# Joining the in-chunk products of a state-space group into one run of column tiles

## The chip, the cores and the metric

The kernel runs on one core of one Trainium2 chip. The metric is the device time of one launch in microseconds (us). Before the change the median of three runs is 729.46 us (729.12, 729.46 and 731.79).

Engines are named as the profile names them: PE multiplies matrices (PEld is its weight load), DVE is the vector engine, ACT the scalar engine, POOL the engine for general work, SP issues the DMAs. Each engine works through its own queue in order and waits at the head of it for what other engines have to deliver. PE writes into eight PSUM banks of 128 partitions by 512 float32 values.

## The reference, cut to what matters

The reference is a two-layer encoder trunk for 512 tokens of width 1024. Layer 0 is a Mamba-2 mixer, layer 1 is differential attention, and a final RMSNorm ends it. The change is in the state-space scan of layer 0:

```python
def step(state, inp):
    x_c, a_c, b_c, c_c = inp
    acs = jnp.cumsum(a_c, axis=1)
    seg = acs[:, :, None] - acs[:, None, :]
    decay = jnp.exp(jnp.where(causal, seg, -jnp.inf))
    cb = jnp.einsum("blgn,bsgn->blsg", c_c, b_c)
    y_diag = jnp.einsum("blsgr,bsgrp->blgrp", cb[..., None] * decay, x_c)
    y_off = jnp.einsum("blgn,bgrpn->blgrp", c_c, state) * jnp.exp(acs)[..., None]
    to_end = jnp.exp(acs[:, -1:] - acs)
    new_state = (state * jnp.exp(acs[:, -1])[..., None, None]
                 + jnp.einsum("blgn,blgrp->bgrpn", b_c, x_c * to_end[..., None]))
    return new_state, y_diag + y_off
```

There are 8 groups with 4 heads of 64 channels each, and a state of 128. `y_diag` is the part inside a chunk, `y_off` is what the state of earlier chunks adds, and `new_state` carries on. Around it stand a projection to z, x, B, C and dt, a causal convolution of four taps on x, B and C, a gate with a grouped norm, and the output projection.

## The kernel before, in words

**Numbers.** Each large product is split into a high and a low part in float32r and made of three matmuls (`mm3`): high by high, high by low, low by high. ACT writes the high part of a weight tile (`whi`) and DVE the low part (`wlo`). The products of the scan itself are plain float32, which the trace shows as two records for each product.

**The stream of dense work.** `stream_a` yields the projections of layer 0 in the order z0 g0 g1 z1 g2 g3 z2 g4 o0 g5 z3 g6 g7 o1 o2 o3. A `g` item (`group_proj`) makes four tiles `pg{g}_0` to `pg{g}_3` (B, C and the two halves of x of one group) in four PSUM banks with the tag "mm". `conv` then works on each: DVE multiplies by the row scale, ACT starts the sum of the four taps, DVE adds the three other taps out of PSUM (`xc<-pg,prc,xc`, shapes 511, 510 and 509), and ACT applies SiLU. The bank of a `pg` tile is free when its last tap (509) is done; then the next item's first matmul can go into it. An `o` item makes 128x512 tiles `po` in the same four banks, and DVE adds each to the residual `x_tok`.

**The scan.** `ssd(g)` is called when the projection of group g is complete. It works on four chunks of 128 tokens. In order of the program:

- C by B for the four chunks into `pcb`, in the one bank with the tag "long"
- transposes of B (`pbt`) and of x (`pxt`); DVE makes `xdt` (x times dt) and `dx` (the skip term), POOL makes `xe` (weighted to the chunk's end)
- DVE multiplies the four heads of the decay tile `dec` by `pcb`, in place
- the states' products `psA` (chunks 0 and 1) and `psB` (chunk 2); ACT, POOL and DVE make the states `hst` of them
- the products inside the chunks, `pyd`: 32 products of 128x64 by 128x64, two for each chunk and head, because the 128 output rows are written as two column tiles of 64. Chunks 0 and 1 fill the bank `pyd{g}_0`, chunks 2 and 3 fill the bank `pyd{g}_1`; DVE adds each bank to `dx`
- the products with the states (`po1`, `po2`, shown as `po<-hst,xc`), DVE scales them into `tmp`, POOL adds them to `dx` for chunks 1 to 3, DVE multiplies by the gate `zs`, ACT squares with a sum, DVE finds the reciprocal root in about ten steps on 128x4 (`v`, `y_i`, `y_y`, `y_c`), ACT scales, PE transposes into `pyt`, and ACT and DVE split the result into `yh` and `yl` for the output projection

All scan tiles but `pcb` come from three banks with the tag "ss". After an odd group, `decays` prepares the `dec` tiles of the next two groups: a 1 MB broadcast DMA, four subtractions and four triangular selections on POOL, and one exponential on ACT. There are two `dec` buffers, so the one of group g+2 is free when the `pyd` products of group g are done.

**What sets the order.** In layer 0 the order on each engine is not written out. The framework's scheduler places every instruction by priority and by its own estimate of a timeline, and interleaves the scan of one group with the dense stream of the next items. Only where the wrapper `Ordered` is switched on (`T.on`, `V.on`, `A.on`) is an instruction kept in program order against the others so marked. Before the change `T.on` is off through the whole scan; it is on from the end of layer 0.

Of the kernel before, what the change touches and what calls it, by code (L numbers as in the profile page):

```python
# [23 lines left out]
R = 4  # L24
# [39 lines left out]
def trunk(ctx, tc, x, x_t, par, w_dt, w_in, w_out, w_kvqg, w_bo, d_skip, lam_qk, fin_g, out):  # L64
    nc = tc.nc
    V, A, T = (Ordered(tc, e) for e in (nc.vector, nc.scalar, nc.tensor))
# [14 lines left out]
    def ss_bank(name):  # L81
        turns[0] += 1
        tag = "mm" if turns[0] % turns[1] >= 3 else "ss"
        return psum.tile([P, 512], F32, tag=tag, name=name, bufs=3 if tag == "ss" else 4)

    def long_bank(name):
        return psum.tile([P, 512], F32, tag="long", name=name)
# [473 lines left out]
    def ssd(g):  # L561
        bc, cc, x0, x1 = conv_out.pop(g)
        xc = (x0, x1)
        dec, een, _ = decs.pop(g)
# [28 lines left out]
        hst = bp.tile([P, 3, R, HD], F32, tag="hst", name=f"hst{g}")  # L593
        hsf = hst.rearrange("p c h e -> p c (h e)")
        psA = ss_bank(f"psA{g}")
        for c in range(2):
            T.matmul(psA[:, c * 256:(c + 1) * 256], lhsT=bt[:, c, :], rhs=xe[:, c].rearrange("p h e -> p (h e)"), start=True, stop=True)
        A.copy(hsf[:, 0], psA[:, 0:256])
# [6 lines left out]

        ss4 = small.tile([P, NQ], F32, tag="ss4", name=f"ss4{g}")
        tmp = bp.tile([P, NQ, R, HD], F32, tag="tmp", name=f"tmp{g}")
        pyd = []
        for q in range(2):
            pyd.append(ss_bank(f"pyd{g}_{q}"))  # L610
            for c in (2 * q, 2 * q + 1):
                for h in range(R):
                    o = (c % 2) * 256 + h * HD

                    for r in (slice(0, 64), slice(64, 128)):
                        T.matmul(pyd[q][r, o:o + HD], lhsT=dec[:, h, c, r], rhs=xdt[:, c, h, :], start=True, stop=True)
            dq = dx[:, 2 * q:2 * q + 2].rearrange("p c h e -> p c (h e)")
            V.tensor_tensor(out=dq, in0=pyd[q].rearrange("p (c e) -> p c e", c=2), in1=dq, op=ALU.add)
        if g % 2 and g < G - 1:
# [35 lines left out]
    for g in range(G):  # L655
        until(f"g{g}")
        if g < G - 1:
            ssd(g)
        else:
            with tc.high_priority():  # L660
                ssd(g)
# [277 lines left out]
    def half(t, n):  # L939
        hs = slice(n * 512, (n + 1) * 512)  # L940
        return x_tok[:, t, hs], fg[:, hs], ot[t][:, hs], out[t * P:(t + 1) * P, hs]
# [59 lines left out]
    h = DH - 1  # L1001
# [59 lines left out]
    y, f, o, dst = half(3, 0)  # L1061
# [71 lines left out]
```

## Time and profile before

| | |
|---|---|
| median of three runs | 729.46 us |
| the profiled execution | 729.15 us, of which the span from the first to the last instruction is 727.0 us |
| granted TensorE clock | 0.998 |
| PE busy | 713.5 us (98%) |
| DVE, ACT, POOL busy | 528.0, 433.7 and 117.7 us |
| `pyd` products | 512 records from 78.2 to 408.4 us |

A row of the timeline has the start in us, the length in us, engine, source line, operation, output tile and inputs, shapes, the count, and in brackets the idle time before it with what ended it. Records of one kind that follow each other are merged into one row. Matmuls are pipelined, so a row's length is longer than the time until the next one starts: a 128x512 product is 0.40 us long, and the next starts 0.23 us after it. The price of work on PE is therefore read from starts, not from lengths. Nearly every instruction has line 55, the line of the wrapper, so groups are told apart by tile names.

### The profile page before, as it was taken

How to read it: one execution, taken by the hardware profiler on the slowest of the kernel's cores; microseconds unless marked ns; L12 is line 12 of the kernel's file. 1: busy time of each engine (PE TensorE's matmuls, PEld its weight loads, DVE VectorE, ACT ScalarE, POOL GpSimd, SP SyncE). 2: the span in 40 equal slices, each digit the busy share in tenths (PEclk: the TensorE clock that was granted, in tenths of full speed). 3: DMA queues.
4: the chain of work that ended last, by engine and by line, in shares of the span. 5: the costliest groups of instructions: out<-in, count | busy, mean ns of one | idle time of the engine just before them, and what ended most of it. 6: DMA issues, size and time to landing. Idle time of an engine off the chain costs nothing.

```text
span 727.0 us, 10819 instructions
## 1 busy us (share of the span) xinstructions
PE 713.5 (98%) x3989; PEld 593.1 (82%) x3989; DVE 528.0 (73%) x1202; ACT 433.7 (60%) x965; POOL 117.7 (16%) x158
## 2 busy tenths in 40 slices
PE   9999999999999999999999999999999999999996
PEld 7787888888888888887788869888988898889874
DVE  4688964979479668569995846657667857785886
ACT  5948573654735527527534348667766756756566
POOL 0108241412315024150110101000000000000002
PEclk9999999999999999999999999999999999999999
DMA  8634313314133231231122310331221131122003
GB/s 302 233 131 162 116 59 117 117 58 175 58 117 116 95 137 60 91 142 59 59 70 105 116 59 9 117 115 59 94 82 58 59 117 59 59 90 85 29 1 115
DMA packets 12916, 70.86 MB, mean 97 GB/s; under 512 B 1728, under 2 KB 2496, under 8 KB 5312
## 3 DMA queue, kind: packets, MB, share of 16 engines
q1 hardware_dynamic: 12576, 69.90, 26.5%
q8 instruction: 31, 0.51, 0.3%
q10 hardware_dynamic: 288, 0.28, 0.1%
q14 instruction: 21, 0.17, 0.1%
HBM read 68.02 MB, written 2.16 MB: 97 GB/s over the span
## 4 chain that ended last, share of the span: by engine, by line
PE 90%; DVE 7%; ACT 1%; issue 1%; POOL 0%; ACTq 0%; DVEq 0%; POOLq 0%
PE pg L55 21%; PE po L55 14%; PE pz L55 12%; PE pt L55 7%; PE pv L55 6%; PE pq L55 6%; PE pk L55 6%; PE pb L55 3%; PE sc L55 3%; PE pyd L55 2%; PE pc L55 2%; DVE wlo L55 2%; DVE xc L55 2%; PE pyt L55 1%; PE pxt L55 1%; PE psA L55 1%
## 5 line engine op out<-in xcount | busy, mean ns | idle before, releaser
L55 DVE SCALAR_TENSOR_TENSOR wlo<-raw,prm,whi 128x512 fp32r<-128x512 f32 (+1 forms) x256 | 150.4, 633 | 52.7 <-ACT whi L55 51.3
L55 ACT ACTIVATE whi<-raw,prm 128x512 fp32r<-128x512 f32 (+1 forms) x256 | 136.8, 606 | 81.4 <-PE pg L55 30.1
L55 PE MATMUL pg<-a_hi,whi 128*128 128x512 f32 x256 | 103.3, 404 | 1.5 <-DVE y_c L55 1.5
L55 PE MATMUL pg<-a_hi,wlo 128*128 128x512 f32 x256 | 102.3, 402 | 0.0
L55 PE MATMUL pg<-a_lo,whi 128*128 128x512 f32 x256 | 102.3, 400 | 0.0
L55 DVE SCALAR_TENSOR_TENSOR xc<-pg,prc,xc 128x511 f32<-128x511 f32 (+2 forms) x96 | 69.6, 738 | 4.8 <-ACT xc L55 4.4
L55 PEld LDWEIGHTS pg<-a_hi,whi 128*128 128x128 f32 x256 | 48.1, 188 | 13.1 <-issue 1.9
L55 PEld LDWEIGHTS pg<-a_hi,wlo 128*128 128x128 f32 x256 | 48.1, 188 | 11.0
L55 PEld LDWEIGHTS pg<-a_lo,whi 128*128 128x128 f32 x256 | 48.1, 188 | 10.7
L55 PE MATMUL po<-whi,yh 128*128 128x512 f32 x128 | 51.4, 402 | 1.5 <-DVE xc L55 0.8
L55 PE MATMUL po<-wlo,yh 128*128 128x512 f32 x128 | 51.1, 399 | 0.0
L55 PE MATMUL po<-whi,yl 128*128 128x512 f32 x128 | 50.4, 398 | 0.0
L55 PE MATMUL pz<-wlo,a_hi 128*128 128x512 f32 x128 | 50.3, 399 | 0.0
L55 PE MATMUL pz<-whi,a_lo 128*128 128x512 f32 x128 | 49.8, 398 | 0.0
L55 PE MATMUL pz<-whi,a_hi 128*128 128x512 f32 x128 | 49.6, 401 | 0.0
L971 POOL TENSOR_TENSOR ot<-ot,fg 128x512 f32<-128x512 f32 x4 | 5.1, 1289 | 256.9 <-ACT ot L55 256.9
L55 ACT ACTIVATE s<-s,mx 128x128 f32<-128x128 f32 (+3 forms) x64 | 35.5, 556 | 9.6 <-DVE mx L55 9.1
L55 ACT ACTIVATE xc<-pg,prc 128x512 f32<-128x512 f32 x32 | 24.6, 773 | 26.6 <-DVE pg L55 26.5
L589 POOL TENSOR_TENSOR xe<-xdt,tok 128x256 f32<-128x256 f32 x24 | 17.3, 749 | 139.6 <-DVE xdt L55 139.6
L55 DVE CUSTOM_DVE_ANT_0 s<-sc,bias 128x128 f32<-128x128 f32 (+3 forms) x64 | 29.4, 488 | 12.2 <-PE sc L55 11.7
L55 ACT ACTIVATE xc<-xc 128x512 f32<-128x512 f32 x32 | 20.0, 629 | 28.3 <-DVE xc L55 28.2
L55 PE MATMUL pv<-whi,b_hi 128*128 128x256 f32 x128 | 36.6, 286 | 0.0
(243 smaller groups left out, 1719.7 us busy)
## 6 DMA issues: line engine op xcount, KB each, us to landing
raw<-in_w_in SPq DMA_DIRECT2D x23, 1024.0 KB, 4.8
raw<-in_w_kvqg SPq DMA_DIRECT2D x16, 1024.0 KB, 4.8
dec<-acs_d SPq DMA_DIRECT2D x8, 1024.0 KB, 4.8
raw<-in_w_out SPq DMA_DIRECT2D x8, 1024.0 KB, 4.8
raw<-in_w_bo SPq DMA_DIRECT2D x4, 1024.0 KB, 4.8
x_tok<-in_x SPq DMA_DIRECT2D x4, 512.0 KB, 9.3
out<-ot SPq DMA_DIRECT2D x7, 256.0 KB, 2.4
raw<-in_w_in SPq DMA_DIRECT2D x4, 256.0 KB, 5.8
```

The costliest lines, as they stand in the source:

```text
L55: i = op(*args, **kw)
L589: GP.tensor_tensor(out=xe[:, c], in0=xdt[:, c], in1=toe_tok[:, c, hs].unsqueeze(2).to_broadcast([P, R, HD]), op=ALU.mult)
L971: GP.tensor_tensor(out=o, in0=o, in1=f, op=ALU.mult)
```

## The change

The products of `ssd` from `psA` to the last of `pyd` are now kept in program order on PE. The second bank of `pyd` no longer comes from the three "ss" banks but is the "long" bank, which `pcb` has held before in the same group. The chunks are taken in the order 2, 3, 0, 1 and the heads from 3 down to 0, all 32 products behind each other; the two additions to `dx` on DVE come after all of them in the program. No product and no other operation is added or taken away.

```diff
         psA = ss_bank(f"psA{g}")
+        T.on = True
         for c in range(2):
             T.matmul(psA[:, c * 256:(c + 1) * 256], lhsT=bt[:, c, :], rhs=xe[:, c].rearrange("p h e -> p (h e)"), start=True, stop=True)
...
         tmp = bp.tile([P, NQ, R, HD], F32, tag="tmp", name=f"tmp{g}")
-        pyd = []
-        for q in range(2):
-            pyd.append(ss_bank(f"pyd{g}_{q}"))
+
+        pyd = [ss_bank(f"pyd{g}_0"), long_bank(f"pyd{g}_1")]
+        for q in (1, 0):
             for c in (2 * q, 2 * q + 1):
-                for h in range(R):
+                for h in reversed(range(R)):
                     o = (c % 2) * 256 + h * HD
 
                     for r in (slice(0, 64), slice(64, 128)):
                         T.matmul(pyd[q][r, o:o + HD], lhsT=dec[:, h, c, r], rhs=xdt[:, c, h, :], start=True, stop=True)
+        T.on = False
+        for q in range(2):
             dq = dx[:, 2 * q:2 * q + 2].rearrange("p c h e -> p c (h e)")
             V.tensor_tensor(out=dq, in0=pyd[q].rearrange("p (c e) -> p c e", c=2), in1=dq, op=ALU.add)
```

Since the scheduler works with the whole program, the order moves on every engine through layer 0, up to the last transposes of group 7. Three places follow.

On PE in group 6, this is the piece of the difference around the first two tiles of the output projection o1 (`po_0_0`, `po_0_1`); `pg_3` is the last tile of the projection of group 7, and numbers tell one tile from another.

```order
 L55 MATMUL pg_3_3051<-a_hi,wlo_2963 128x512
-L55 MATMUL psB_3109<-xe_3094,bt_3076 128x256
-L55 MATMUL pyd_0_3115<-xdt_3078,dec_2683 64x64 x16
 L55 MATMUL po_0_0_3348<-whi_3054,yh_1539 128x512
 L55 MATMUL po_0_0_3348<-wlo_3055,yh_1539 128x512
```

```order
 L55 MATMUL po_0_0_3348<-whi_3054,yl_1868 128x512
+L55 MATMUL psA_3103<-xe_3094,bt_3076 128x256 x2
+L55 MATMUL psB_3109<-xe_3094,bt_3076 128x256
+L55 MATMUL pyd_1_3116<-xdt_3078,dec_2683 64x64 x16
+L55 MATMUL pyd_0_3115<-xdt_3078,dec_2683 64x64 x16
 L55 MATMUL po_0_1_3498<-whi_3054,yh_1539 128x512
```

```order
 L55 MATMUL po_0_1_3498<-whi_3054,yl_1868 128x512
-L55 MATMUL pcb_3352<-xc_3291,xc_3272 128x128 x4
-L55 MATMUL pyd_1_3133<-xdt_3078,dec_2683 64x64 x16
-L55 MATMUL po_3151<-hst_3102,xc_3003 128x256
 L55 MATMUL po_0_2_3512<-whi_3054,yh_1539 128x512
```

Before, the two halves of `pyd` stood 24 products of `po` apart; now both stand together between `po_0_0` and `po_0_1`, with the states' products ahead of them. In the same stretch the eight transposes `pxt` of group 6 moved from the products of `pg_0` to those of `pg_3`.

On DVE behind group 5, these are the rows from the root of group 5's norm (`v`, `y_i`, `y_y`, `y_c`) to the last tap of the convolution on the first tile of group 6 (`xc_2984<-pg_0_2896`, 509). Before:

```order
L55 TENSOR_TENSOR pg_0_2896<-pg_0_2896,ar_row 128x512
L55 TENSOR_SCALAR v_2741<-ss_2645 128x4
L55 TENSOR_SCALAR y_i<-v_2741 128x4
L55 TENSOR_SCALAR y_y<-y_i 128x4
L55 TENSOR_TENSOR y_c<-y_y,v_2741 128x4
L55 TENSOR_TENSOR y_c<-y_c,y_y 128x4
L55 TENSOR_TENSOR pg_1_2897<-pg_1_2897,ar_row 128x512
L55 SCALAR_TENSOR_TENSOR xc_2984<-pg_0_2896,prc,xc_2984 128x511
L55 SCALAR_TENSOR_TENSOR y_c<-y_c 128x4
L55 SCALAR_TENSOR_TENSOR xc_2984<-pg_0_2896,prc,xc_2984 128x510
L55 SCALAR_TENSOR_TENSOR y_y<-y_c,y_y 128x4
```

and now:

```order
L55 TENSOR_TENSOR pg_0_2896<-pg_0_2896,ar_row 128x512
L55 TENSOR_TENSOR tmp_2646<-po_2725,tok 128x512
L55 SCALAR_TENSOR_TENSOR xc_2984<-pg_0_2896,prc,xc_2984 128x511
L55 SCALAR_TENSOR_TENSOR xc_2984<-pg_0_2896,prc,xc_2984 128x510
L55 TENSOR_TENSOR pg_1_2897<-pg_1_2897,ar_row 128x512
L55 SCALAR_TENSOR_TENSOR xc_2984<-pg_0_2896,prc,xc_2984 128x509
```

Before, a tap of the second tile (`xc_3003`) and then the 509 tap followed the last row shown. Now the 509 tap ends the rows shown, and the root starts behind nine of the twelve taps of group 6.

On ACT at the end of layer 0, this is the piece of the difference from group 7's copy of the first state to its scaling; `tmp,ss<-dx` are the four squares, and `whi_3746` is the weight split of the next layer's first tile.

```order
 L55 COPY hst_3387<-psA_3388 128x256
-L55 ACTIVATE tmp_3399,ss_3398<-dx_3364 128x256 x3
-L55 ACTIVATE whi_3746<-raw_3744,prm 128x256 x5
-L55 ACTIVATE tmp_3399,ss_3398<-dx_3364 128x256
-L55 ACTIVATE whi_3746<-raw_3744,prm 128x256 x3
+L55 ACTIVATE tmp_3399,ss_3398<-dx_3364 128x256 x4
+L55 ACTIVATE whi_3746<-raw_3744,prm 128x256 x8
 L55 ACTIVATE tmp_3399<-dx_3364,y_y 128x256 x4
```

Before, the fourth square stood behind five weight splits; now all four squares come first. On POOL, after groups 0 to 5, the subtractions for the decay tile that becomes free now stand ahead of the second and third addition to `dx` of the same group; before they stood behind them in four of the six.

## The prediction

> **What bounds the kernel now.** I read the page first: the busy shares and the chain of waits.
>
> ```profile
> span 727.0 us, 10819 instructions
> PE 713.5 (98%) x3989; PEld 593.1 (82%) x3989; DVE 528.0 (73%) x1202; ACT 433.7 (60%) x965; POOL 117.7 (16%) x158
> PE 90%; DVE 7%; ACT 1%; issue 1%; POOL 0%; ACTq 0%; DVEq 0%; POOLq 0%
> ```
>
> PE is busy for 98% of the span and holds 90% of the chain. A change can win in two ways only: PE spends less on the same products, or one of its few waits goes. So the second view is the list of what PE waited for.
>
> ```profile
> PE pg L55 <- DVE y_c L55: 1.5, 1, 1.5
> PE po L55 <- DVE xc L55: 0.8, 1, 0.8
> PE pyt L55 <- ACT tmp L55: 0.7, 1, 0.7
> PE pxt L55 <- ACT xc L55: 0.6, 1, 0.6
> PE po L55 <- ACT yh L55: 0.6, 1, 0.6
> ```
>
> These five waits of layer 0 (total, times, longest, all in us) are single events. The fourth lies in group 0, ahead of the first instruction that moves, and the fifth is the way from the last transposes into the last output tiles, whose order is the same. The first three can change.
>
> The third view is the timeline of PE around the `pyd` runs of group 0, with the row of all `pyd` records (length at least, median and most in ns).
>
> ```profile
> 78.24 1.15 PE L55 MATMUL pyd<-xdt,dec 128*64 128x64 f32 x32
> 79.33 0.50 PE L55 MATMUL pg<-a_hi,whi 128*128 128x512 f32 x1
> 79.66 0.40 PE L55 MATMUL pg<-a_lo,whi 128*128 128x512 f32 x1
> ...
> 83.86 0.40 PE L55 MATMUL pg<-a_lo,whi 128*128 128x512 f32 x1
> 84.09 0.40 PE L55 MATMUL pg<-a_hi,wlo 128*128 128x512 f32 x1
> 84.42 1.15 PE L55 MATMUL pyd<-xdt,dec 128*64 128x64 f32 x32
> 85.50 1.56 PE L55 MATMUL po<-hst,xc 128*128 128x256 f32 x6
> ```
>
> ```profile
> L55 PE MATMUL pyd<-xdt,dec x512: 222/222/270, 78.2 to 408.4; 128*64 128x64 f32 x171
> ```
>
> The reader is to see the edges of a run. A 128x512 product is followed by the next after 0.23 us (83.86 to 84.09), but after 0.33 us when a run of `pyd` comes next (84.09 to 84.42). The first product behind a run also takes 0.33 us (79.33 to 79.66).
>
> **The change part by part. First, the run's edges.** The run is 1.15 us long and its last record 0.22 us, so 31 steps take 0.93 us: 0.03 us for one record, 0.96 us for 32. From its start to the next product's start a run takes 1.08 us (84.42 to 85.50), so leaving costs 0.12 us. With 0.10 us on entering and 0.10 us on the first product after it, one run costs 0.32 us beyond its products. The change makes one run of 64 records out of two of 32 in each of eight groups: 8 x 0.32 = 2.6 us. All of it is on PE and nothing hides it. Low end: if the seam in the joined run, where the second bank's first product waits for semaphores anew, costs an entry of 0.10 us, 8 x 0.22 = 1.8 us stay. High end: if a run's first steps are slower than its mean, as one record of 270 ns beside a median of 222 suggests, some 0.05 us more, 3.0 us in all. I take 2.6, since the steps come from the mean of a whole run.
>
> The page "TensorEngine Tiling (Array Packing)" of the Trainium skill, section "Tiling Modes", says that changing the tiling mode drains the TensorE, and changing only the tile does not. By that rule the seam, which keeps the mode, costs nothing, and the saving would be the full price of a run; by the other reading the seam pays an entry. The page has no figure for a drain.
>
> **The second bank and the order of heads** cost nothing if the products never wait for `dec` or for the "long" bank. Group 0 is the tightest: its decay tiles are multiplied by `pcb`, which also empties that bank, long before 78.24.
>
> ```profile
> 65.59 2.48 DVE L55 TENSOR_TENSOR dec<-dec,pcb 128x512 f32<-128x512 f32 x4 [0.78 <-ACT dec L55]
> ```
>
> That ends at 68.07, 10.2 us ahead. Behind the waiting product the whole stream of PE would stand, so the cover matters; it would have to shrink by these 10 us.
>
> **The first wait (PE on the bank of group 6's first tile).** This is the timeline behind group 5, all engines.
>
> ```profile
> 320.94 4.92 POOL L553 TENSOR_TENSOR dec<-dec,tok 128x512 f32<-128x512 f32 x4
> ...
> 322.85 0.69 DVE L55 TENSOR_TENSOR pg<-pg,ar_row 128x512 f32<-128x512 f32 x1
> ...
> 323.89 0.97 DVE L55 TENSOR_SCALAR y_i<-v 128x4 int32<-128x4 int32 x1
> ...
> 324.90 0.98 DVE L55 TENSOR_SCALAR y_y<-y_i 128x4 int32<-128x4 int32 x1
> ...
> 326.97 0.69 DVE L55 TENSOR_TENSOR pg<-pg,ar_row 128x512 f32<-128x512 f32 x1
> ...
> 328.69 0.40 PE L55 MATMUL pg<-a_hi,wlo 128*128 128x512 f32 x1
> ...
> 329.07 1.40 DVE L55 SCALAR_TENSOR_TENSOR xc<-pg,prc,xc 128x511 f32<-128x511 f32 x2
> ...
> 330.62 0.47 PE L55 MATMUL pg<-a_hi,whi 128*128 128x512 f32 x1 [1.53 <-DVE y_c L55]
> ```
>
> PE would have gone on at 328.69 + 0.23 = 328.92 and went on at 330.62: 1.7 us late. The name `y_c` is only the next DVE instruction. What PE needs is the 509 tap of `pg_0`, the second of the two in the row of 329.07, which ends at 330.47. It is late because between the multiply of `pg_0` (to 323.54) and that of `pg_1` (326.97) DVE works 3.4 us on five steps of the norm's root, two of them of nearly 1 us on 128x4 while POOL subtracts. In the changed order these steps stand behind the tap. Behind the multiply of `pg_0` come `tmp`, two taps, the multiply of `pg_1` and the 509 tap: 0.69 + 0.70 + 0.70 + 0.69 + 0.70 = 3.5 us, and 0.2 us because ACT's part of the convolution is a little longer than `tmp`. The tap ends at 323.54 + 3.7 = 327.2, 1.7 us before PE asks. I take the whole 1.7 us as gone. Bounds: 1.7 and 0.0, the latter if POOL's subtractions, which also come earlier now, hold DVE up by the same 3.4 us at the weight splits ahead. What is late instead is the root of group 5; its transposes have moved too, in among the products of group 7's first tile.
>
> **The second wait (PE on the bank of group 7's second tile).**
>
> ```profile
> 355.84 1.02 PE L55 MATMUL psA<-xe,bt 128*128 128x256 f32 x4
> ...
> 361.20 0.40 PE L55 MATMUL po<-whi,yl 128*128 128x512 f32 x1
> 361.56 0.73 DVE L55 SCALAR_TENSOR_TENSOR xc<-pg,prc,xc 128x509 f32<-128x509 f32 x1
> ...
> 362.43 0.47 PE L55 MATMUL po<-whi,yh 128*128 128x512 f32 x1 [0.83 <-DVE xc L55]
> ```
>
> ```profile
> 353.18 1.28 DVE L55 TENSOR_TENSOR pg<-pg,ar_row 128x512 f32<-128x512 f32 x2
> 354.38 4.01 DVE L55 SCALAR_TENSOR_TENSOR xc<-pg,prc,xc 128x511 f32<-128x511 f32 x6
> ```
>
> `po_0_1` was due at 361.43 and started at 362.43, 1.0 us late, behind the tap that ends at 362.29. DVE rows take 0.67 us each here (4.01 / 6). Before, 14 rows follow `pg_1`'s multiply up to that tap, 9.4 us from 353.18. In the changed order DVE has 15 rows there, 10.0 us, but ahead of the multiply only `pg_0`'s, a weight split and two `yl`, 4 x 0.67 = 2.7 us, while PE takes 12 x 0.23 = 2.8 us for `pg_1`: it can take the tile up at once. PE now has between `pg_1` and `po_0_1` 36 products of 0.23 (8.3 us), the states' products (1.3 us, six passes of some 0.22) and both halves of `pyd` (2.0 us), 11.6 us without the eight transposes. That leaves 1.6 us. I take 1.0 us as gone; if DVE is again some 2.5 us late with `pg_1`, 0.9 us come back, so the bounds are 0.1 and 1.0.
>
> **The third wait (the last transposes on group 7's scaling).**
>
> ```profile
> 411.92 1.01 DVE L55 TENSOR_TENSOR tmp<-po,tok 128x256 f32<-128x256 f32 x2
> ...
> 415.46 2.10 ACT L55 ACTIVATE whi<-raw,prm 128x256 fp32r<-128x256 f32 x5
> ...
> 417.46 0.40 ACT L55 ACTIVATE tmp<-dx 128x256 f32<-128x256 f32 x1
> ...
> 420.40 0.40 PE L55 MATMUL po<-whi,yl 128*128 128x512 f32 x1
> ...
> 421.52 1.63 PE L55 MATMUL pyt<-ident,tmp 128*128 128x128 f32 x8 [0.72 <-ACT tmp L55]
> ```
>
> Due at 420.63, started at 421.52: 0.9 us late. The chain runs over the fourth square, which ACT does after five weight splits of 2.1 us. Now the squares come first (2.1 us earlier), and ten more products stand between the end of `pyd` and the transposes (2.3 us more room). Against it, the state products of chunks 2 and 3 stand 13 products behind `pyd` instead of at once (3.0 us), and eight splits instead of three run between the squares and the scaling, about 0.5 us longer than the root takes. Net 0.9 us, just enough; since it has no reserve I take 0.7, bounds 0 and 0.9.
>
> The DMA queue keeps its order on SP. The decay tiles' DMAs start earlier with the earlier end of `pyd`, and POOL's work with them.
>
> **The sum.** 2.6 + 1.7 + 1.0 + 0.7 = 6.0 us. The profiled execution took 729.15 us, 2.1 us of them outside its span of 727.0, which nothing here touches; it is 0.3 us below the median of 729.46. So 723.2 us for such an execution and 723.5 us by the median.
>
> **The rivals.** *The run's edges alone (726.9 us).* DVE stays as late as it was because POOL's work, moved earlier, holds it at other places, or new waits of the same size appear where a scheduler's estimate was wrong. For it speaks that three waits of about 1 us in 400 us are what is left of many near misses; against it, the worked margins of 1.7 and 1.6 us. Then only 2.6 us go: 729.46 - 2.6 = 726.9.
>
> *Slower: POOL's queue holds DVE (737 us).* In all of groups 0 to 5 POOL now subtracts for the next decay tile before it adds chunks 2 and 3 to `dx`, and DVE's gate multiply for chunk 2 waits for that in order, with the taps of the next tiles behind it.
>
> ```profile
> 325.81 2.40 POOL L554 TENSOR_SCALAR_AFFINE_SELECT dec<-dec 128x512 f32<-128x512 f32 x4
> ```
>
> ```profile
> dec<-acs_d SPq DMA_DIRECT2D x8, 1024.0 KB, 4.8
> ```
>
> From the end of `pyd`: 4.8 us to land, 4.92 us to subtract, one selection of 0.6 us (2.40 / 4) and the addition: 11 us before DVE can go on. In group 5 DVE has 16 rows ahead of that multiply, 10 to 11 us at 0.67. It decides from the point where the stand exceeds the margin of 1.7 us. If all six exceed it by what the first wait was, 6 x 1.7 = 10 us come on, and the first three terms win nothing but the edges: 729.46 - 2.6 + 10 = 737.
>
> The page "SBUF — State Buffer" of the Trainium skill, section "Who interferes with whom", speaks for this rival: DVE and GpSimd share a port pair, and whoever starts first holds it for its whole instruction. This trace agrees: `y_i` and `y_y` took 0.97 and 0.98 us beside the subtractions of 1.23 us each.
>
> *No effect (728.5 us).* The scheduler's interleaving gives back on PE what the edges save, by more waits under 0.3 us. Little speaks for it, as PE's records show almost none now.
>
> **How the numbers follow.** The forecast has 0.60, the edges alone 0.27, no effect 0.08, slower 0.05. The predicted time is the forecast's, 723.5 us. Its own bounds are 6.6 us (3.0 + 1.7 + 1.0 + 0.9) and 3.7 us gained (the edges and one of the three waits), 722.9 to 725.8; the range reaches on to the edges alone with the low price (729.46 - 1.8 = 727.7) and, below, 1 us past the forecast's own end for waits that I don't see: 721.8 to 728.0. About 0.5% is what a measurement of this kernel can tell from no change, 3.6 us, so faster means under 725.8: 0.62, with a little of the second case; within 0.5%: 0.33; slower: 0.05.
>
> **What would show it.** Right: eight runs of 64 `pyd` records, each some 2.0 us from its start to the next product, and no step of 0.33 us in the middle; no wait of PE on a tap behind groups 5 and 6; the transposes of group 7 after at most 0.3 us of waiting. Wrong: a row of PE waits in layer 0 that names DVE or POOL with over 1 us, above all the DVE gate multiply standing idle for POOL in groups 0 to 5; or a joined run that costs 2.2 us, which would mean that the price is not at the edges.

## The result

The changed kernel takes 722.25 us in the median of four runs (721.62 to 722.50), the kernel before beside it 730.0 us. The ratio is 0.989, with a 95% interval of 0.9868 to 0.9911: faster by 1.1%. The profiled execution took 722.47 us with a span of 720.7 us, 6.3 us less than the span before. The medians lie further apart (7.75 us) than the two spans: the launches of the kernel before, taken beside the experiments, differ in granted clock (729.9 us in mean at 0.998 and above, 731.6 us at 0.995 and below), and the four of the changed kernel all have 0.998 or 0.999. These are the first rows of the page after the change, and its row on the chain of waits:

```profile
span 720.7 us, 10835 instructions
PE 709.7 (98%) x3989; PEld 592.5 (82%) x3989; DVE 519.9 (72%) x1202; ACT 433.8 (60%) x965; POOL 113.7 (16%) x158
PE 95%; DVE 3%; ACT 1%; issue 0%; POOL 0%; ACTq 0%; POOLq 0%
```

PE still has the same 3989 records and holds 95% of the chain where it held 90%. DVE is busy for 8 us less with the same 1202 instructions, and POOL for 4 us less with the same 158. Most of DVE's difference lies in the 128x4 rows of the norm's roots: before, 15 of their 169 rows overlapped a POOL instruction and took 8.6 us together, where rows of that size take 0.14 to 0.17 us each otherwise; in the changed kernel none overlaps one. That is some 6 of the 8 us.

The list of what PE waited for, after the change (total, times, longest, in us):

```profile
PE pxt L55 <- ACT xc L55: 1.2, 1, 1.2
PE po L55 <- ACT yh L55: 0.6, 1, 0.6
```

The waits on the bank of group 6's first tile (1.5), on group 7's second tile (0.8) and of the last transposes (0.7) are gone from it. The wait of group 0's transposes `pxt` is 1.2 us, where it was 0.6.

Group 0 on PE, from the states' products to the dense work behind the run:

```profile
77.74 0.59 PE L55 MATMUL psB<-xe,bt 128*128 128x256 f32 x2
78.26 2.08 PE L55 MATMUL pyd<-xdt,dec 128*64 128x64 f32 x64
80.28 0.50 PE L55 MATMUL pg<-a_hi,whi 128*128 128x512 f32 x1
80.61 0.40 PE L55 MATMUL pg<-a_lo,whi 128*128 128x512 f32 x1
```

The run of 64 records takes 2.02 us from its start to the next product (78.26 to 80.28). Two runs of 32 took 1.08 us each, 2.16 us. The difference of 0.14 us comes on top of what lies outside the runs: one entry of 0.09 to 0.10 us and one late first product of 0.10 us less. That is 0.35 us for a group and 2.8 us for eight groups. The second half pays no entry: the step from record 32 to record 33 is 0.05 us, like the others.

Behind group 5, this is DVE in the changed kernel from the multiply of group 6's first tile on:

```profile
318.56 0.69 DVE L55 TENSOR_TENSOR pg<-pg,ar_row 128x512 f32<-128x512 f32 x1
319.16 0.68 DVE L55 TENSOR_TENSOR tmp<-po,tok 128x512 f32<-128x512 f32 x1
320.10 1.53 DVE L55 SCALAR_TENSOR_TENSOR xc<-pg,prc,xc 128x511 f32<-128x511 f32 x2 [0.26 <-ACT xc L55]
321.55 0.69 DVE L55 TENSOR_TENSOR pg<-pg,ar_row 128x512 f32<-128x512 f32 x1
322.14 0.74 DVE L55 SCALAR_TENSOR_TENSOR xc<-pg,prc,xc 128x509 f32<-128x509 f32 x1
```

The last tap (509) ends at 322.88, 4.3 us after its tile's multiply began. Before, it ended 7.6 us after (322.85 to 330.47). PE asks for the bank 4.0 us later and goes on without a wait:

```profile
326.91 0.40 PE L55 MATMUL pg<-a_hi,whi 128*128 128x512 f32 x1
```

At the end of layer 0 the transposes of group 7 come 0.39 us behind the product ahead of them, 0.16 us late, where they were 0.89 us late:

```profile
414.81 0.40 PE L55 MATMUL po<-whi,yl 128*128 128x512 f32 x1
415.20 1.64 PE L55 MATMUL pyt<-ident,tmp 128*128 128x128 f32 x8
```

### The profile page after: what moved, and what is told of

It is laid out like the page before. It is cut to its first block, busy times and chain, and to the rows that moved or that the text cites. A ratio compares the mean times of both kernels' runs of the same rounds, so it can differ in the third digit from the quotient of the medians.

```text
span 720.7 us, 10835 instructions
## 1 busy us (share of the span) xinstructions
PE 709.7 (98%) x3989; PEld 592.5 (82%) x3989; DVE 519.9 (72%) x1202; ACT 433.8 (60%) x965; POOL 113.7 (16%) x158
## 3 DMA queue, kind: packets, MB, share of 16 engines
HBM read 68.02 MB, written 2.16 MB: 97 GB/s over the span
## 4 chain that ended last, share of the span: by engine, by line
PE 95%; DVE 3%; ACT 1%; issue 0%; POOL 0%; ACTq 0%; POOLq 0%
PE pg L55 23%; PE po L55 16%; PE pz L55 12%; PE pt L55 7%; PE pv L55 6%; PE pq L55 6%; PE pk L55 6%; PE pb L55 3%; PE sc L55 3%; PE pyd L55 2%; PE pc L55 2%; PE pyt L55 1%; PE pxt L55 1%; PE psA L55 1%; DVE xc L55 1%; PE pcb L55 1%
## 5 line engine op out<-in xcount | busy, mean ns | idle before, releaser
L55 PEld LDWEIGHTS pg<-a_hi,wlo 128*128 128x128 f32 x256 | 48.1, 188 | 10.9
L589 POOL TENSOR_TENSOR xe<-xdt,tok 128x256 f32<-128x256 f32 x24 | 14.1, 615 | 166.8 <-DVE xdt L55 166.8
L55 PE MATMUL pv<-wlo,b_hi 128*128 128x256 f32 x128 | 35.7, 279 | 0.0
```

Of the source, the lines that this page charges most:

```text
L55: i = op(*args, **kw)
L589: GP.tensor_tensor(out=xe[:, c], in0=xdt[:, c], in1=toe_tok[:, c, hs].unsqueeze(2).to_broadcast([P, R, HD]), op=ALU.mult)
```

## The experiments

The question was which part of the gain belongs to the joining itself, and which to the order that the scheduler made with it. Eleven kernels were run. For each, one sum was worked out from PE's records in the profiled execution, from PE's first record to the last transpose of layer 0: a step from one start to the next that is over 0.2 us longer than usual for its shape (0.234 us for 512 columns, 0.216 for 256, 0.111 for 128x128) counts with its excess as a wait, and what is left is called the rest. Delays under 0.2 us are part of the rest.

| kernel | median, us | ratio to before, 95% interval | `pyd` runs | waits, us | rest, us |
|---|---|---|---|---|---|
| before | 730.0 | | 16 | 5.0 | 416.4 |
| changed | 722.25 | 0.9868 to 0.9911 | 8 | 1.7 | 413.4 |
| e1 seam | 728.16 | 0.996 to 0.9982 | 16 | 4.7 | 416.0 |
| e4 own bank | 731.97 | 1.0005 to 1.0037 | 16 | 7.4 | 417.0 |
| e6 taps first | 732.91 | 1.0018 to 1.0047 | 16 | 6.5 | 416.2 |
| e7 no tiles | 733.73 | 1.0029 to 1.0062 | 8 | 2.4 | 423.4 |
| e5 forward | 724.06 | 0.9896 to 0.9932 | 8 | 3.2 | 413.4 |
| e3 no pin | 728.05 | 0.996 to 0.9991 | 21 | 0.8 | 419.5 |
| e9 bank alone | 735.06 | 1.0047 to 1.0101 | 29 | 3.9 | 421.6 |
| e8 small subtract | 727.62 | 0.995 to 0.9981 | 17 | 3.9 | 416.1 |
| e12 heads forward | 722.36 | 0.9867 to 0.9922 | 8 | 1.7 | 413.2 |
| e10 two queues | 721.75 | 0.9863 to 0.9911 | 8 | 1.7 | 413.7 |
| e11 transposes joined | 721.81 | 0.9865 to 0.9909 | 8 | 0.7 | 413.6 |

The rest goes by the number of runs. A line through the twelve kernels with column tiles is 410.2 us plus 0.39 us for each run, and the farthest lies 1.0 us off it. The waits do not go by the number of runs: 0.8 us with 21 runs, 3.2 us with 8.

Three of the profiles hold a half-clock stretch: 3.4 us at a granted clock of 0.5, in which PE works on eight to ten records. They are e4 from 332.1 us, inside layer 0, e6 from 425.3 us and e9 from 428.2 us, both behind it. From the last transposes to the end it is 306.3 us in e6 and 305.6 us in e9, and 304.1 to 304.2 us in all the others. So some 2 us of e6 and 1.5 us of e9 are neither edges nor waits. Each of the three stretches begins within 3 us behind a wait of PE of over 1 us, but other waits as long have none behind them, and what brings it is not shown.

### A seam in the joined run (e1)

```diff
-        T.matmul(psB[:, 0:256], ...)          # ahead of both halves
         for q in (1, 0):
+            if q == 0:
+                T.matmul(psB[:, 0:256], ...)  # between the halves
             for c in (2 * q, 2 * q + 1):
```

The two instructions on POOL and DVE that make the third state out of `psB` move with it in the program.

> The changed kernel with the product psB taken out from ahead of the joined run and put between its two halves, so that each group has two runs of 32 records again, only one product apart. Bank, pinning and order of heads stay as changed. Theory (edges): a second run costs its entry and its exit wherever the halves stand, 8 x 0.33 = 2.7 us, so 725.0 us against 722.25 us of the changed kernel; each half some 1.08 us from its start to the next product, the records behind psB and behind the first half 0.10 us late each. Rival (order alone): the gain of the change is the order it gives to DVE and the transposes, and the number of runs is by the way; then 722.3 us, since the taps stay ahead of the root here.

Measured: 728.16 us, 3.2 us above what the theory said. Group 0 on PE, and what PE waited for:

```profile
77.12 1.15 PE L55 MATMUL pyd<-xdt,dec 128*64 128x64 f32 x32
78.20 0.70 PE L55 MATMUL psB<-xe,bt 128*128 128x256 f32 x2
78.83 1.15 PE L55 MATMUL pyd<-xdt,dec 128*64 128x64 f32 x32
79.91 0.50 PE L55 MATMUL pg<-a_hi,whi 128*128 128x512 f32 x1
80.25 0.40 PE L55 MATMUL pg<-a_lo,whi 128*128 128x512 f32 x1
```

```profile
PE psA L55 <- POOL xe L589: 1.1, 2, 0.5
PE pz L55 <- DVE xc L55: 0.7, 1, 0.7
PE po L55 <- DVE xc L55: 0.7, 1, 0.7
```

The edges came as expected. From the first `pyd` to the second product behind the runs it is 3.13 us (77.12 to 80.25). In the changed kernel it is 2.35 us (78.26 to 80.61), and the two `psB` records, which stand inside here, take 0.43 us of their own; 3.13 - 2.35 - 0.43 = 0.35 us for each group. The rest in the table rose by 2.6 us. But new single waits came too, at places where neither the kernel before nor the changed one waits: the states' products of groups 2 and 6 on POOL's `xe`, the first product behind the run of the same groups, and one addition to `x_tok` at 233 us, 3.9 us in all by the steps. So the theory was right on the edges, and the rival is right that the order counts for as much.

### The second half in a bank of its own (e4)

```diff
-        pyd = [ss_bank(f"pyd{g}_0"), long_bank(f"pyd{g}_1")]
+        pyd = [ss_bank(f"pyd{g}_0"), ss_bank(f"pyd{g}_1")]
```

> The changed kernel with the second half's products in a bank of the three ss banks again; pinning and the reversed order stay. The halves come apart again, by some 20 dense products. Theory (edges and waits): 2.7 us of edges come back, and since DVE has the root of group 5 ahead of the taps again, so does the first wait of 1.7 us: 722.25 + 2.7 + 1.7 = 726.7 us, up to 729 if the second and third wait come back too. Rival (pinning is what wins): the bank is worth nothing and the time stays within 1 us of 722.25.

Measured: 731.97 us, 5.3 us above the theory, and far from the rival. Pinning and reversing alone win nothing. The list of waits:

```profile
PE pg L55 <- DVE y_c L55: 2.1, 1, 2.1
PE pyt L55 <- ACT tmp L55: 1.6, 1, 1.6
```

The edges are back (rest 417.0, some of it from the half-clock stretch), and with the root of group 5 ahead of the taps the first wait is back too, at the same place and longer (2.1 us, before 1.5), as is the wait of the last transposes (1.6 us, before 0.7). The expected sum took them at their old sizes, and had none of the others (its full list also has 1.2 us in group 0 and 0.9 us behind a run).

### The taps ahead of the root, in the kernel before (e6)

```diff
+    late = {5: small.tile([P, NQ], F32, name="late", bufs=1)}
     def conv(ps, ft, name, bufs):
...
         cw = [prc[:, at + k:at + k + 1] for k in range(4)]
+        if ft == 22:                                   # group 6, first tile
+            GP.tensor_copy(late[5][:, 0:1], cw[0])
+            cw[0] = late[5][:, 0:1]                    # read by its 509 tap
...
-        v4 = small.tile([P, NQ], F32, tag="v4", ...)   # first step of the root
+        v4 = late.get(g) or small.tile([P, NQ], F32, tag="v4", ...)
```

Everything in `ssd` from this step on, the scaling and the transposes too, is called for group 5 only when the projection of group 6 is complete.

> The kernel before, two runs and three ss banks as they were, with one thing held: the root of group 5's norm starts only behind the last tap of group 6's first tile (its first step writes a tile that this tap reads; one POOL copy of 128x1 is added, and the rows of group 5's end are later in the program). Theory (single waits): the first wait of 1.7 us goes alone, and with it nothing of the edges: 730.0 - 1.7 = 728.3 us, and no PE wait in the list of waits on the bank of group 6's first tile. Down to 727.3 if the moved transposes also clear the second wait. Rival (the wait moves on): DVE has the same work in all, so PE waits for a later tap or for the transposes of group 5 instead, 730.0 us.

Measured: 732.91 us, 4.6 us above the theory. The wait on group 6's first tile did go, but all of layer 0 takes 1.3 us longer than before, and behind it come the 2 us of the half-clock stretch. In the place of the first wait:

```profile
PE pyt L55 <- ACT tmp L55: 2.7, 1, 2.7
PE po L55 <- DVE x_tok L55: 1.1, 1, 1.1
```

One of the new waits lies where the edit changes no order: the 1.1 us on `x_tok` comes at 232 us, between groups 3 and 4, where the order on every engine is that of the kernel before but for the early copy on POOL. There POOL and DVE stand like this, first in this kernel, then in the kernel before:

```profile
225.72 5.55 POOL L558 TENSOR_TENSOR dec<-dec,tok 128x512 f32<-128x512 f32 x4
...
226.17 1.27 DVE L55 TENSOR_TENSOR dx<-dx,zs 128x256 f32<-128x256 f32 x1
227.36 2.99 DVE L55 SCALAR_TENSOR_TENSOR wlo<-raw,prm,whi 128x512 fp32r<-128x512 f32 x2
```

```profile
226.44 0.41 DVE L55 TENSOR_TENSOR dx<-dx,zs 128x256 f32<-128x256 f32 x1
226.77 1.40 DVE L55 SCALAR_TENSOR_TENSOR wlo<-raw,prm,whi 128x512 fp32r<-128x512 f32 x2
...
227.65 4.47 POOL L553 TENSOR_TENSOR dec<-dec,tok 128x512 f32<-128x512 f32 x4
```

POOL's subtractions began 1.9 us earlier here, and DVE's multiply and two splits beside them took 4.3 us instead of 1.8. DVE came to the addition 2.2 us later, and PE waited. So a wait of 1 us can come from when the decay tile lands, with the order unchanged. What made the last transposes 2.7 us late was not taken apart.

### No column tiles (e7)

```diff
-                    for r in (slice(0, 64), slice(64, 128)):
-                        T.matmul(pyd[q][r, o:o + HD], lhsT=dec[:, h, c, r], rhs=xdt[:, c, h, :], ...)
+                    T.matmul(pyd[q][:, o:o + HD], lhsT=dec[:, h, c, :], rhs=xdt[:, c, h, :], ...)
```

> The changed kernel with each product of a chunk and head as one product of 128 output rows instead of two column tiles of 64: half as many records, the same results, no tile mode at all. Theory (the edges are changes of tile mode): no record is 0.10 us late on the way into or out of a run. The time then hangs on the step of a 128x64 record of float32: if it is half of the 0.11 us that the records of 128x128 float32 take, 32 x 0.055 = 1.8 us for a group, as now, and 8 x 0.33 = 2.7 us are won, 719.5 us; if the step stays at 0.11 us because of the weights, 32 x 0.11 = 3.5 us, 8 x 1.25 = 10 us are lost, 732 us. Rival (the edges come from the semaphores that the first product waits for, or from a change of shape): the entry and the exit stay 0.10 us late, and the time is 2.7 us above what the step gives.

Measured: 733.73 us, the upper of the two cases. Group 0 on PE:

```profile
77.56 0.59 PE L55 MATMUL psB<-xe,bt 128*128 128x256 f32 x2
77.99 3.68 PE L55 MATMUL pyd<-xdt,dec 128*128 128x64 f32 x32
81.48 0.48 PE L55 MATMUL pg<-a_hi,whi 128*128 128x512 f32 x1
81.80 0.40 PE L55 MATMUL pg<-a_lo,whi 128*128 128x512 f32 x1
```

A record of 128 rows by 64 columns steps in 0.11 us, as one of 128x128 does. From the first `pyd` to the second product behind the run it is 3.81 us (77.99 to 81.80), where it is 2.35 us in the changed kernel. Eight times the difference, less eight entries of 0.09 us, is 10.9 us; the rest rose by some 10. The edges are what this experiment is for. The two `psB` records take 0.43 us here (77.56 to 77.99), where they take 0.52 us ahead of column tiles: the entry is gone. The 3.81 us less one usual step of 0.23 us leave 3.58 us, and 32 records of 0.1116 us are 3.57 us: nothing is left over for the first steps, the leaving and the product behind. That product does take 0.32 us (81.48 to 81.80), but the first and the last record of the run are shorter by as much (0.055 and 0.084 us). The same holds behind other short float32 records: the last of the 128x128 transposes `pxt` steps in 0.03 us and the 512-column product behind it in 0.315 us, together the usual 0.11 + 0.23. So the whole price of a run beyond its products, 0.35 us, belongs to the column tiles. The theory was right on this and low by 1.7 us on the time, and the rival is out.

### Both halves in forward order (e5), and only the heads (e12)

```diff
-        for q in (1, 0):           # e5 alone
+        for q in (0, 1):           # e5 alone
             for c in (2 * q, 2 * q + 1):
-                for h in reversed(range(R)):
+                for h in range(R):
```

> The changed kernel with the chunks in the order 0, 1, 2, 3 and the heads from 0 up again; one joined run in each group, the bank and the pinning as changed. Theory A (a joined run wins 8 x 0.35 us of edges, and because the products of a group then end together, the work of DVE and POOL behind them moves as well, so that the single waits go): 722 to 723.5 us, with no PE wait over 1 us behind group 0. Theory B (the edges are sure, but where PE waits is decided anew by each order that the scheduler makes, as the kernel with the seam showed, where 3.9 us of new waits came beside 2.8 us of edges): 723.5 to 727 us, with PE waits of 0.7 to 2 us at other places than before.

> The changed kernel with the heads from 0 up again; the second half still comes first. The scheduler gives every engine the same order as in the changed kernel, so this shows what the reversed heads are worth, and how much of a wait list is one launch's own. Theory (the heads' order is by the way): 722.3 us within 0.7 us, PE's waits in layer 0 the same but for the wait of group 0's transposes, which was 0.6 to 1.6 us or absent in the profiles so far. Rival (the forward kernel lost its 1.8 us by the heads, not by the halves): 724 us, with the wait of 1.4 us on group 6's first tile.

Measured: 724.06 us for the forward kernel and 722.36 us with the heads alone turned back. The heads are by the way. The halves are not: the forward kernel has the joined run and the same rest (413.4), and a wait of 1.4 us at the old place, behind group 5. First the work ahead of the multiply, on POOL and on DVE, then DVE from the multiply on:

```profile
315.89 5.43 POOL L553 TENSOR_TENSOR dec<-dec,tok 128x512 f32<-128x512 f32 x4
...
317.41 4.45 DVE L55 SCALAR_TENSOR_TENSOR wlo<-raw,prm,whi 128x512 fp32r<-128x512 f32 x3
321.79 0.69 DVE L55 TENSOR_TENSOR pg<-pg,ar_row 128x512 f32<-128x512 f32 x1
323.32 0.75 DVE L55 SCALAR_TENSOR_TENSOR xc<-pg,prc,xc 128x511 f32<-128x511 f32 x1 [0.85 <-ACT xc L55]
323.99 0.63 DVE L55 TENSOR_TENSOR dx<-dx,zs 128x256 f32<-128x256 f32 x1
...
325.14 0.84 DVE L55 TENSOR_TENSOR dx<-dx,zs 128x256 f32<-128x256 f32 x1
325.90 2.05 DVE L55 SCALAR_TENSOR_TENSOR xc<-pg,prc,xc 128x510 f32<-128x510 f32 x3
```

```profile
326.32 0.40 PE L55 MATMUL pg<-a_hi,wlo 128*128 128x512 f32 x1
328.09 0.47 PE L55 MATMUL pg<-a_hi,whi 128*128 128x512 f32 x1 [1.37 <-DVE v L55]
```

The root is behind the taps here, but two things bring the wait back. Both gate multiplies (`dx<-dx,zs`) stand among the taps, so the 509 tap ends at 327.95, 6.2 us after the multiply began (4.3 us in the changed kernel). And the multiply came late: the three splits ahead of it took 4.45 us beside POOL's subtractions, where three take 2.07 us in the changed kernel, and it began 4.8 us ahead of 326.56, where PE asked (8.4 us there). By these numbers either alone would have left no wait: 4.8 covers 4.3, and 8.4 covers 6.2. That is reckoned and not run. Theory B holds in its time, though the largest wait is at the old place and not at another: joining the run doesn't of itself take the waits away.

### Without the pinning (e3), and the bank alone (e9)

```diff
-        T.on = True     # e3: the change without these two lines
-        T.on = False
```

```diff
-            pyd.append(ss_bank(f"pyd{g}_{q}"))                             # e9: the kernel before
+            pyd.append((long_bank if q else ss_bank)(f"pyd{g}_{q}"))
```

> The changed kernel without the pinning of the products' order on PE; the bank shared with C by B and the reversed order stay. The scheduler now puts some products of the second half ahead of and between the states' products, which makes 21 runs in the eight groups instead of 8. Theory (each run costs its edges): 13 x 0.35 = 4.5 us more than the changed kernel, 726.8 us, with no new waits; each piece late by 0.09 us on entering and by 0.10 us on leaving. Rival (pinning is by the way, the bank is what wins): 722 to 723 us.

> The kernel before with one part of the change: the bank of the second half is the one shared with C by B. No pinning, chunks and heads in the old order. The scheduler then splits the second half around the states' products and around the first half, 29 runs in the eight groups instead of 16. Theory (edges by the number of runs): 13 x 0.35 = 4.5 us more than before, 734.5 us, or 731 us if the products' common end takes away the three single waits. Rival (what counts is that the halves are close together, whatever the number of runs): 723 to 726 us.

Measured: 728.05 and 735.06 us, 1.3 and 0.6 us above what the number of runs was to give. Group 0 on PE without the pinning:

```profile
75.90 0.33 PE L55 MATMUL pyd<-xdt,dec 128*64 128x64 f32 x2
76.16 0.70 PE L55 MATMUL psA<-xe,bt 128*128 128x256 f32 x2
...
77.22 1.96 PE L55 MATMUL pyd<-xdt,dec 128*64 128x64 f32 x58
```

Two records of `pyd` by themselves take 0.26 us (75.90 to 76.16), where they take 0.06 us inside a run. With 21 runs the rest is 419.5 us, 6.1 us above the changed kernel, of which 13 runs at 0.35 us explain 4.6; the waits are among the fewest (0.8 us). With 29 runs it is 421.6 us, 5.2 us above the kernel before, and 1.5 us more come behind layer 0 from the half-clock stretch. So the bank alone makes the kernel slower than before: the scheduler breaks the second half up into pieces. With the order of the halves changed as well (e3) a small gain is left, 0.2% with an interval of 0.1 to 0.4. Without the pinning most of the gain is lost.

### Smaller subtractions on POOL, in the kernel before (e8)

```diff
-                GP.tensor_tensor(out=dec[:, h], in0=dec[:, h], in1=..., op=ALU.subtract)           # 128x512
+                GP.tensor_tensor(out=dec[:, h, :, 0:8], in0=dec[:, h, :, 0:8], in1=..., ...)        # 128x32
```

> The kernel before with POOL's subtractions for the decay tiles cut from 128x512 to 128x32 each (the rest of the tile is left unsubtracted, so the decays are other numbers); on DVE the root of group 5 stays ahead of the last tap of group 6's first tile. Theory (the first wait is DVE's rows of the root lengthened beside POOL: 0.97 and 0.98 us where such rows take 0.17 us alone): the rows shrink, the first wait of 1.7 us goes or falls under 0.3 us, DVE's busy time falls by some 10 us, and the time is 728.3 us or a little less. Rival (the wait comes from the order on DVE alone): PE still waits 1 us or more on the first tile's bank, 730 us.

Measured: 727.62 us, 0.7 us under the theory, with 519.1 us of DVE instead of 528.0. The root behind group 5, which stands ahead of the taps as before:

```profile
322.86 0.69 DVE L55 TENSOR_TENSOR pg<-pg,ar_row 128x512 f32<-128x512 f32 x1
...
323.90 0.55 DVE L55 TENSOR_SCALAR y_i<-v 128x4 int32<-128x4 int32 x1
...
326.14 0.15 DVE L55 TENSOR_TENSOR y_c<-y_c,y_y 128x4 f32<-128x4 f32 x1
...
327.76 0.75 DVE L55 SCALAR_TENSOR_TENSOR xc<-pg,prc,xc 128x509 f32<-128x509 f32 x1
```

```profile
323.20 2.40 POOL L554 TENSOR_SCALAR_AFFINE_SELECT dec<-dec 128x512 f32<-128x512 f32 x4
```

The multiply starts at the same time as before (322.86 and 322.85), and the tap ends at 328.51 instead of 330.47, ahead of 328.92, where PE asked for the bank before (329.50 in this launch). The wait is gone with the root still in front, though PE waits 0.5 us on the next tile's bank instead. The row `y_i` took 0.97 us beside subtractions of 1.23 us, it takes 0.55 us beside selections of 0.60 us, and rows of that size take 0.15 us when POOL is idle. One tap of the second tile, which stood ahead of the 509 tap before, stands behind it here; that is 0.7 us of the 2.0, so the shorter rows are the other 1.3, and they alone would have left some 0.4 us of the 1.7.

### The wait that is left: two queues (e10), and joined transposes (e11)

```diff
-        nc.sync.dma_start(acs_d[:, c, :], acs[c * H:(c + 1) * H, :])                        # e10
+        (nc.sync, nc.scalar)[c % 2].dma_start(acs_d[:, c, :], acs[c * H:(c + 1) * H, :])
```

```diff
-        for j in range(2):                                                                  # e11
+        for j in (1, 0):
             pxt = ss_bank(f"pxt{g}_{j}")
+            T.on = True
             for c in range(NQ):
                 T.transpose(pxt[:, c * P:(c + 1) * P], xc[j][:, c * P:(c + 1) * P], ident)
+            T.on = False
```

> The changed kernel with two of the four small writes of the summed decays issued by ACT instead of SP; PE, DVE and POOL keep their order. It tests the one long wait left in layer 0, the transposes of x in group 0 (1.2 us in the changed kernel, absent with forward order and with the seam): POOL's first copy of the decay tile came at 54.9 us where the wait is there and at 52.9 us where it isn't, and ACT does the exponential of that tile ahead of the SiLU that the transposes need. Theory (the issues of 0.44 us one behind the other are part of that path): two at a time bring the tile 0.9 us forward, the wait shrinks to some 0.4 us and the time to 721.4 us. Rival (the write's landing sets it, or ACT is late with its two issues): POOL's copy stays at 54 to 55 us and the time at 722.3 us or above.

> The changed kernel with the transposes of x pinned as well, the second half ahead of the first. In group 0 both halves then stand together some 13 products later than the first stood; elsewhere they stood together already. Theory (the wait of the transposes in group 0 is the only one of over 1 us left, and 3 us of products now cover it): it goes, 722.25 - 1.3 = 721.0 us. Rival (what comes behind, POOL's weighting and DVE's multiplies of the decay tile, is late next): a wait of PE on the states' products or on the first product of the joined run of group 0, 722 to 724 us.

Measured: 721.75 and 721.81 us, neither to be told from the changed kernel's 722.25. POOL's first copy of group 0's decay tile in the changed kernel, in the kernel with two queues and in the forward kernel:

```profile
54.92 0.20 POOL L551 COPY dec<-dec 128x8 f32<-128x8 f32 x1 [25.47 <-DMA dec<-acs_d]
```

```profile
55.14 0.20 POOL L551 COPY dec<-dec 128x8 f32<-128x8 f32 x1 [26.02 <-DMA dec<-acs_d]
```

```profile
52.90 0.19 POOL L551 COPY dec<-dec 128x8 f32<-128x8 f32 x1 [23.62 <-DMA dec<-acs_d]
```

With two queues SP issued the broadcast behind the small writes at 47.84 instead of 50.12, yet POOL's copy is no earlier and the wait is 1.1 us: in this profile it is the landing of the broadcast that sets it, and the theory of the issues fails. The median lies between theory and rival and can't decide. In the forward kernel the order up to there is the same, the copy is 2 us earlier, and there is no wait at all. In the profile with joined transposes the wait is gone (the waits fall by 1.0 us to 0.7), but its copy came at 53.45, one of the early ones, and with those no kernel waits there, joined or not. So it is not shown that joining the transposes takes the wait out.

## Why the prediction was right

**The edges: 2.6 us predicted, 2.8 us by the records, 3.0 us by the rest (416.4 to 413.4).** The step was right and a little small. The working took the run's steps from their mean, 0.03 us; but the first pair steps in 0.10 us where later ones take 0.05, so each run has 0.05 us more of its own and the price is 0.35 us, not 0.32. That was the upper bound's reason. The seam cost nothing, as the section "Tiling Modes" of the Trainium skill's page "TensorEngine Tiling (Array Packing)" has it, since the mode stays. The page's rule that a change of mode drains the array agrees with the run without column tiles, where nothing of the 0.35 us is left.

**The bank and the heads at nothing.** The heads: shown, 722.36 against 722.25 us. The bank: no product of the run waits for it. But it is not free in every arrangement: alone, without the pinning, it makes layer 0 4.1 us longer.

**The first wait, 1.7 us: gone.** The tap ends 3.6 us after the end of its tile's multiply (319.25 to 322.88), where the working had 3.7. It named two reasons for the old wait, the root's place and its rows lengthened beside POOL. The small subtractions show that most of it goes with shorter rows and the root still in front. The reserve was larger than worked out, 4.0 us instead of 1.7, because the multiply began 8.4 us ahead of PE's question where it began 6.1 us ahead before. That was not forecast, and here it was not needed: with the old lead of 6.1 us the 1.7 us would have been left. But the lead can also shrink. In the forward kernel the mechanism of the lower bound came, POOL's subtractions beside the splits ahead, and together with two gate multiplies among the taps it brought the wait back. **The second, 1.0 us: gone. The third, 0.7 us: 0.73 us gone** (0.89 to 0.16).

**The fourth wait, said to be ahead of what moves and so the same:** it was 0.77 us by the step and is 1.34 now. Nothing that moved did it. With group 0's transposes at the same place in PE's order, the profiles of the experiments show it at 1.2 to 1.8 us or not at all, and where it is absent the decay tile was 2 us earlier. The prediction took one launch's value for a fixed one. That it did not spoil the sum was luck: PE came to it 0.58 us earlier in this launch.

**The sum, 6.0 us:** by the spans 6.3. By the table 3.0 of rest and 3.3 of waits. The median came out 1.25 us under the forecast: 0.3 us of it lies in the span, 0.4 us outside it (2.15 us before, 1.8 now, forecast to be the same), and the rest in which launch is profiled and which is the median. The lower of the prediction's own bounds, 3.7 us, does not come out as the edges and one of the three waits (2.6 with 1.0 or 1.7 is 3.6 or 4.3); nothing rests on it.

**The rivals.** "The edges alone" fell for this kernel, by its 3.3 us of waits, but the edges are all that the joining is sure of: the forward kernel, with 8 runs and the same rest, keeps 3.2 us of waits and stands 1.8 us above the changed one. "POOL's queue holds DVE" did not come: in the changed kernel DVE stands 0.37 us for POOL ahead of one gate multiply behind group 5, and PE doesn't wait. The part of its mechanism that is true is the gate multiplies ahead of the taps and the splits beside POOL (e5), once and with 1.4 us, not six times. "No effect" fell.

So half of the gain was priced by a rule that held within 1.0 us in all twelve kernels with column tiles. The other half was read from the order on DVE, rightly for this order, but it hangs on that order and on when a tile lands; the chance of 0.27 for its failing was not too much.

What stays open: why the last of the small writes of the decays lands 3.3 us after its issue in the changed kernel (46.72 to 50.04) and 1.5 us after it in the forward kernel (46.70 to 48.20), with the decay tile 2 us later for it; what made the last transposes so late in e4 and e6; what brings the half-clock stretches; and the 0.04 us by which the line through the table is above the records' price of a run.

## What to carry to other kernels

Price a change of the order on the full engine in two parts. The part that lies in the engine's own steps (entering, leaving, the first product behind) can be taken from starts of records and held in every arrangement here. It has to be taken over the whole run with its neighbours, since a late product behind can be the other side of a short record ahead. The part that lies in its waits belongs to one order of the other engines and has to be looked up there again after each edit, however small. To join two runs, pin both: a shared bank without pinning gave the scheduler pieces to spread and made the kernel slower. Which half goes first changed nothing in the joined run itself, only the order of the other engines.

## What the runs showed of the hardware

- A float32 record of 128 rows by 64 columns steps in 0.11 us, like one of 128 columns; two column tiles of 64 rows side by side step in 0.06 us for the pair.
- A run of column tiles among full float32 products costs 0.35 us beyond its records (0.09 on entering, 0.05 on the first pair, 0.10 on leaving, 0.10 on the first product behind); a run of 32 records without column tiles costs nothing beyond them, though the 512-column product behind it steps in 0.32 us, because its own first and last record step in 0.055 and 0.084 us instead of 0.11.
- DVE's rows beside POOL are lengthened by up to one POOL instruction: a 128x4 row takes 0.15 us alone, 0.55 beside a selection of 0.60, 0.97 beside a subtraction of 1.23, and three weight splits took 2.07 us with POOL idle (the changed kernel) and 4.45 beside subtractions (e5). The page "SBUF — State Buffer" of the Trainium skill, section "Who interferes with whom", has the lock held for the whole instruction, and these lengths agree. POOL is lengthened as well: the same four subtractions took 4.08 us behind group 5 in the changed kernel, 5.55 beside two splits in e6.
- The kernel's one wait of over 1 us in group 0 depends on the launch: the same order waits 1.2 us with the decay tile at 54.9 us and not at all with it at 52.9 us.
- The granted clock can fall to 0.5 for 3.4 us in the middle of a kernel with PE busy: in e6 and e9 the part behind the last transposes takes 306.3 and 305.6 us with such a stretch in it, 304.1 to 304.2 us without.
